# Keys of both attentions in parts of 72, 72 and 128, and the indexer's heads issued in pairs

## The chip, the cores and the metric

The kernel runs on one core of a Trainium2 chip. The metric is the device time of one execution in microseconds (us). TensorE (PE in the profile) multiplies; its weight loads have rows of their own (PEld). VectorE (DVE), ScalarE (ACT) and GpSimd (POOL) do the rest, and SyncE (SP) issues the weight transfers.

## The reference, cut to what matters

A decoder block works on 272 positions, 16 meta tokens and 256 real ones. A sparse attention and a forgetting attention, 8 heads of 128 each, run in parallel; a mixture of 16 experts follows. For the real positions it comes to:

```python
# sparse attention (A): the indexer scores the keys, the best 68 stay
dots  = einsum('bqhd,bsd->bqhs', qi, ki)              # 16 heads of 64
score = einsum('bqh,bqhs->bqs', wi, relu(dots)) * 64 ** -0.5
_, sel = lax.top_k(where(causal, score, NEG), 68)
ya = softmax(q @ k_sel.T * 128 ** -0.5) @ v_sel       # 8 heads
# forgetting attention (B): all earlier keys, with a decay
yb = softmax(where(causal, q @ k.T * 128 ** -0.5 + cq - c, NEG)) @ v
merged = sigmoid(ga) * (ya @ w_branch_a) + sigmoid(gb) * (yb @ w_branch_b)
h = h + merged @ w_out
h = h + hier_moe(h)                                   # 16 experts
```

## The kernel before

Weights come as pieces of 1 MB by SP's queue (`Stream.load`). In the projections each half of a piece is split by ACT (`whi`, line 132) and DVE (`wlo`, line 133), and `projT` (line 286) issues three products for each tile of 128 weight columns. Every `projT` step ends in `tick()`, and `later(d, f)` puts `f` into the tick `d` steps on. So indexer and attentions stand on TensorE's queue in small blocks between blocks of 24 projection products (48 between two ticks in which attention B has work). A scheduler behind the program orders each engine's instructions by what is ready. A float32 product counts as two passes in the profile, each with its weight load; a transpose and a product of a split operand count as one.

The **indexer** (`index_dots`, line 509): `qiT` holds the queries of two heads of 64 on the two partition halves, and `kiT` holds the keys twice. A dot product of query tile `t` (0 or 1) and head `h` contracts over 64 partitions, those of the half `h % 2`, and streams 144 keys (`t` = 0) or 272 (`t` = 1). ACT takes the relu, DVE adds it into `score[t]`. Tick `1 + i` issues head `i` for both query tiles, so both products of a tick use the same half. PSUM has two buffers (`psx`), which lie in different banks.

The **attentions** (`attention`, line 545) go through 16 steps (2 query tiles of 8 heads), each of three parts in following ticks (every second tick in B): `s1` makes logits (`pqk`) and the softmax on DVE and ACT (lines 557 to 562); `s2` transposes the probabilities into one PSUM tile (`ppt`) and ACT copies them to SBUF; `s3` multiplies by the values into `pav`. The 272 keys are cut into the 16 meta tokens and two blocks of 128; query tile 0 sees 16 + 128 keys, tile 1 all three parts. The first product of `s3` therefore contracts over 16 partitions (`vm`, `pTm`), the others over 128. The values are brought into that form by `v_out` (line 478), again with transposes of 128, 128 and 16 columns. The meta values of both attentions share the tile `vmeta`, on partitions 0 to 15 and 32 to 47.

After the attentions come the rest of the gated projections, the output projection (`wo`), the routing, and the experts (`up_unit`, `down_unit`), whose weights use 11 and later 12 more buffers.

Of the kernel before, what the change touches and what calls it, by code (L numbers as in the profile page):

```python
# [8 lines left out]
F32 = mybir.dt.float32  # L9
# [4 lines left out]
AF = mybir.ActivationFunctionType  # L14
# [7 lines left out]
TOPK = 68  # L22
EPS = 1e-6
NEG = -1e30
TAKEN = -3e38
CAP = 64
SPLITS, LOOK = 5, 3
# [122 lines left out]
def hybrid_block(ctx, tc, a):  # L150
    nc = tc.nc
    V, S, T = nc.vector, nc.scalar, nc.tensor
# [7 lines left out]
    U1 = ctx.enter_context(tc.tile_pool(name="units", bufs=4))  # L160
    ph1 = ExitStack()
    U2 = ph1.enter_context(tc.tile_pool(name="units2", bufs=9))
    tmp = ph1.enter_context(tc.tile_pool(name="tmp", bufs=1))

    def unit(shape, dt, name, pool=U1):
        return pool.tile(shape, dt, name=name, tag="u")

    def pj(shape, name="pj"):
        return ps.tile(shape, F32, name=name, tag="pj", bufs=4)

    def psx(shape, name="psx"):
        return ps.tile(shape, F32, name=name, tag="psx", bufs=2)

    def pt(shape, name="pt"):
        return ps.tile(shape, F32, name=name, tag="pt", bufs=1)

    def pv(shape, name="pv"):
        return ps.tile(shape, F32, name=name, tag="pv", bufs=1)

    def mm(out, lhsT, rhs, start, stop):  # L180
        T.matmul(out, lhsT, rhs, start=start, stop=stop, skip_group_check=True)  # L181
# [26 lines left out]
    ident = const.tile([128, 128], F32, name="ident")  # L208
# [20 lines left out]
    def row272(rows=128):  # L229
        return tmp.tile([128, L], F32, name="row", tag="row", bufs=5)[:rows]  # L230
# [37 lines left out]
    def later(d, f, *args):  # L268
        clock[1] += 1
        todo.append((clock[0] + d, clock[1], f, args))  # L270
# [36 lines left out]
    rrow = tmp.tile([128, L], F32, name="rrow")  # L307
# [109 lines left out]
    foxr = tmp.tile([104, L], F32R, name="foxr")  # L417
# [35 lines left out]
    causal = [tmp.tile([128, NK[t]], F32, name=f"causal{t}") for t in range(2)]  # L453
    for t in range(2):
        V.tensor_scalar(causal[t], jp[:, :NK[t]], 16 + 128 * t, NEG, op0=OP.is_gt, op1=OP.mult)

# [7 lines left out]
    for j in range(4):  # L464
        p = projT(16, xreal, 256)
# [2 lines left out]


    kaT = unit([128, 8, L], F32, "kaT", U2)  # L470
    va = unit([128, 2, 1024], F32, "va", U2)
    vmeta = tmp.tile([48, 1024], F32, name="vmeta")
    vam, vbm = vmeta[0:16], vmeta[32:48]

    def cks(k):
        return ckT[0][:, k, :], ckT[1][:, k, :]

    def v_out(c, p, v, vm, row):

        o = row272()  # L480
        if row is None:
            V.tensor_copy(o, p)
        else:
            V.tensor_tensor(o, p, row, op=OP.mult)
        hs = slice(c * 128, c * 128 + 128)

        def tr():
            q = (pv if c % 2 else pt)([128, 3, 128], "pvt")
            for t in range(2):
                T.transpose(q[:, t, :], o[:, 16 + t * 128:144 + t * 128], ident)  # L490
            T.transpose(q[:16, 2, :], o[:, 0:16], ident)
            S.activation(v[:, :, hs], q[:, 0:2, :], AF.Copy)
            S.activation(vm[:, hs], q[:16, 2, :], AF.Copy)
        later(1, tr)

    for j in range(4):
        p = projT(4, cks, L)
        for i in range(2):
            ropeT_to(kaT[:, 2 * j + i, :], p[i], ropeT[0], ropeT[1], 64)
    for j in range(4):  # L500
        p = projT(4, cks, L)
        for i in range(2):
            v_out(2 * j + i, p[i], va, vam, None)


    score = [tmp.tile([128, 4 + NK[t]], F32, name=f"score{t}") for t in range(2)]
    maskA = [tmp.tile([128, NK[t]], F32, name=f"maskA{t}") for t in range(2)]
# [11 lines left out]
    def topk_round(t):  # L519
        m = tmp.tile([128, 8], F32, name="max8", tag="max8", bufs=2)  # L520
        V.max(m, score[t])
        V.match_replace(score[t], m, score[t], TAKEN)

    def topk_mask(t):
        V.tensor_scalar(maskA[t], score[t][:, 4:], 0.5 * TAKEN, NEG, op0=OP.is_gt, op1=OP.mult)
        V.tensor_tensor(maskA[t], maskA[t], causal[t], op=OP.add)
# [1 line left out]
    for t in range(2):  # L528
        V.memset(score[t][:, 0:4], 3e38)
    for i in range(16):  # L530
        later(1 + i, index_dots, 0, i)
        later(1 + i, index_dots, 1, i)
    for t in range(2):
        for r in range(9):
            later(18 + r // 2 + 5 * t, topk_round, t)
# [2 lines left out]
    qaT = unit([128, 8, 256], F32, "qaT", U2)  # L538
    for j in range(4):
        p = projT(16, xreal, 256)  # L540
# [1 line left out]
            ropeT_to(qaT[:, 2 * j + i, :], p[i][:, :256], tabq[0], tabq[1], 64)  # L542


    def attention(qT, kT, v, vm, masks, yTh, yTl, extra, start, step, mb):
        n = 0
        accs = {}
        for t in (0, 1):
            for h in range(8):
                def s1(t=t, h=h):  # L550
                    nk = NK[t]
                    p = psx([128, L], "pqk")
                    mm(p[:, :nk], qT[:, h, t * 128:(t + 1) * 128], kT[:, h, :nk], True, extra is None)
                    if extra is not None:
                        mm(p[:, :nk], extra[0](t, h), extra[1][:, :nk], False, True)
                    lg = row272()
                    V.tensor_tensor(lg[:, :nk], p[:, :nk], masks[t], op=OP.add)
                    st4 = tmp.tile([128, 4], F32, name="st4", tag="st4", bufs=4)
                    V.tensor_reduce(st4[:, 0:1], lg[:, :nk], axis=AX.X, op=OP.max, negate=True)
                    S.activation(lg[:, :nk], lg[:, :nk], AF.Exp, bias=st4[:, 0:1], accum_out=st4[:, 1:2])  # L560
                    V.reciprocal(st4[:, 2:3], st4[:, 1:2])
                    V.tensor_scalar(lg[:, :nk], lg[:, :nk], st4[:, 2:3], None, op0=OP.mult)
                    later(step, s2, t, h, lg)

                def s2(t, h, lg):
                    q = pt([128, 3, 128], "ppt")
                    T.transpose(q[:16, 0, :], lg[:, 0:16], ident)
                    for b in range(t + 1):
                        T.transpose(q[:, 1 + b, :], lg[:, 16 + b * 128:144 + b * 128], ident)
                    pT = tmp.tile([128, 2, 128], F32, name="pT", tag="pT", bufs=2)  # L570
                    pTm = tmp.tile([48, 128], F32, name="pTm", tag="pTm", bufs=2)[mb:mb + 16]
                    S.activation(pTm, q[:16, 0, :], AF.Copy)
                    S.activation(pT[:, :t + 1, :], q[:, 1:2 + t, :], AF.Copy)
                    later(step, s3, t, h, pT, pTm)

                def s3(t, h, pT, pTm):
                    if h % 4 == 0:
                        accs[t] = pv([128, 4, 128], "pav")
                    o = accs[t][:, h % 4, :]
                    hs = slice(h * 128, h * 128 + 128)  # L580
                    mm(o, vm[:, hs], pTm, True, False)
                    for b in range(t + 1):
                        mm(o, v[:, b, hs], pT[:, b, :], False, b == t)
                    if h % 4 == 3:
                        g, c = slice(h - 3, h + 1), slice(t * 128, t * 128 + 128)
                        S.activation(yTh[:, g, c], accs[t], AF.Copy)
                        V.tensor_tensor(yTl[:, g, c], accs[t], yTh[:, g, c].bitcast(F32), op=OP.subtract)
                later(start + n * step, s1)
                n += 1

    def y_parts(n, pool):
        return unit([128, 8, 256], F32R, n + "h", pool), unit([128, 8, 256], F32R, n + "l", pool)


    vb = unit([128, 2, 1024], F32, "vb")
    for j in range(4):
        p = projT(16, xall, L)
        for i in range(2):
            v_out(2 * j + i, p[i], vb, vbm, rrow)
    yaTh, yaTl = y_parts("ya", U1)  # L600
    attention(qaT, kaT, va, vam, maskA, yaTh, yaTl, None, 1, 1, 0)

    kbT = unit([128, 8, L], F32, "kbT", U2)
    for j in range(4):
        p = projT(16, xall, L)
        for i in range(2):
            V.tensor_tensor(kbT[:, 2 * j + i, :], p[i], rrow, op=OP.mult)
    qbT = unit([128, 8, 256], F32, "qbT")
    for j in range(4):
        p = projT(16, xreal, 256)  # L610
# [8 lines left out]
        return o  # L619

    ybTh, ybTl = y_parts("yb", U2)
    attention(qbT, kbT, vb, vbm, causal, ybTh, ybTl, (fox_lhs, foxr), 1, 2, 32)
    merged = [unit([128, 8, 256], F32, f"merged{i}", U2) for i in range(2)]
    mTh, mTl = [], []

# [33 lines left out]
    tmp = ctx.enter_context(tc.tile_pool(name="tmp2", bufs=1))  # L659
# [50 lines left out]
    for j in range(4):  # L710
        cs = slice(j * 512, (j + 1) * 512)
        p = [pj([128, 512]) for _ in range(2)]
# [34 lines left out]
    lg = sm([2, 24], "lgr")  # L747
    V.memset(lg[:, :, 20:24], TAKEN)
    for t in range(2):
        V.scalar_tensor_tensor(lg[:, t, 0:20], pr[:, t, :], rh[:, t:t + 1], brb, op0=OP.mult, op1=OP.add)  # L750

    def best(src, name):
# [4 lines left out]
        for t in range(2):  # L757
# [8 lines left out]
    V.tensor_tensor(ng, i4, g4, op=OP.not_equal)  # L766
    V.scalar_tensor_tensor(lge.rearrange("p t (g e) -> p t g e", g=4), ng[:, :, :, None].to_broadcast([128, 2, 4, 4]), TAKEN,
                           lg[:, :, 0:16].rearrange("p t (g e) -> p t g e", g=4), op0=OP.mult, op1=OP.add)
# [69 lines left out]
    hs = {}  # L838
# [113 lines left out]
    for kind, n, i in UNITS:  # L952
        if kind == "u":
            g, j = n // 4, n % 4 * 4 + i
# [46 lines left out]
    with tc.If(more > 0):  # L1001
        with tc.tile_pool(name="fb", bufs=1) as fb:
# [3 lines left out]
            q = pt([128, 256], "pfr")  # L1006
# [12 lines left out]
            with tc.For_i(0, 16, 1) as e:  # L1019
# [4 lines left out]
                for s in range(2):  # L1024
                    p = [pj([128, 2, 256], "pfh") for _ in range(2)]
# [91 lines left out]
```

## Time and profile before

| | |
|---|---|
| median of 3 runs | 1250.81 us (1250.37 to 1253.12) |
| profiled execution | 1254.03 us, its span 1252.4 us |
| PE busy | 1198.1 us (96%) |
| PEld, DVE, ACT busy | 70%, 47%, 37% of the span |
| mean bandwidth | 265 GB/s |

The busy share of PE tells which engine to look at, not whether it works at full rate: a pass that waits for its weights counts as busy. What a block costs is read from the starts of the passes in the timeline.

### The profile page before, as it was taken

To read this page: it belongs to the slowest core of one execution; us is meant where nothing else is said; L and a number is where in the kernel's file an instruction comes from. 1 tells how busy PE (TensorE), PEld (TensorE's weight loads), DVE (VectorE), ACT (ScalarE), POOL (GpSimd) and SP (SyncE) were. 2 spreads that over 40 slices of the span, in tenths; PEclk is the share of its full clock that TensorE was granted. 3 is DMA by queue.
4 is the path that set the end of the run, shared out by engine and by line. 5 is a ranking of instruction groups with operands and counts; after the bars stand their busy time and mean duration, and the time that the engine had idled before them with its cause. 6 is when DMAs were issued, how large, how long until landed. Compare 5 with 4: busy or idle time off the path is not lost.

```text
span 1252.4 us, 18527 instructions
## 1 busy us (share of the span) xinstructions
PE 1198.1 (96%) x7602; PEld 878.7 (70%) x7602; DVE 593.5 (47%) x1075; ACT 461.4 (37%) x792; POOL 23.9 (2%) x31
## 2 busy tenths in 40 slices
PE   6999999999999999999999998999999999999994
PEld 6999889999999999999998875443433343333331
DVE  7768868555555655566564435232313131211212
ACT  6567644444355654444444324221211121000013
POOL 1000000000000000000000000000000000000002
PEclk9999999999999999999999998999999999999997
DMA  7554334433543444555559944999999999999992
GB/s 259 199 175 166 135 135 169 160 110 112 179 182 139 148 152 152 185 193 178 200 192 422 383 156 159 420 422 421 420 422 421 420 420 422 422 422 421 421 401 71
DMA packets 48456, 331.41 MB, mean 265 GB/s; under 512 B 5584, under 2 KB 6240, under 8 KB 9200
## 3 DMA queue, kind: packets, MB, share of 16 engines
q1 hardware_dynamic: 47088, 324.88, 66.2%
q0 software_dynamic: 1136, 5.29, 1.1%
q8 instruction: 62, 1.02, 0.3%
q14 instruction: 26, 0.21, 0.0%
q10 hardware_dynamic: 144, 0.01, 0.0%
HBM read 325.96 MB, written 4.19 MB: 264 GB/s over the span
## 4 chain that ended last, share of the span: by engine, by line
PE 92%; ACT 3%; DVE 3%; issue 1%; DMA 1%; SPq 0%; ACTq 0%
PE pj L181 50%; PE pgu L181 19%; PE py L181 10%; PE pxg L181 3%; PE pco L181 3%; PE pav L181 2%; PE pidx L181 1%; PE pqk L181 1%; ACT yh L916 1%; DVE yl L917 1%; PE prt L181 1%; DMA raw<-in_w 1%; ACT xTh L255 1%; PE psm L181 0%; DVE act L891 0%
## 5 line engine op out<-in xcount | busy, mean ns | idle before, releaser
L133 DVE TENSOR_TENSOR wlo<-raw,whi 128x1024 fp32r<-128x1024 f32 (+1 forms) x227 | 276.9, 1223 | 196.6 <-ACT whi L132 195.4
L181 PE MATMUL pj<-xTh,whi 128*128 128x256 f32 (+1 forms) x1216 | 348.0, 286 | 9.9 <-ACT xTh L255 9.9
L132 ACT ACTIVATE whi<-raw 128x1024 fp32r<-128x1024 f32 (+1 forms) x227 | 237.9, 1053 | 324.2 <-PE pj L181 297.1
L181 PE MATMUL pj<-xTl,whi 128*128 128x256 f32 (+1 forms) x1216 | 343.7, 283 | 0.0
L181 PE MATMUL pj<-xTh,wlo 128*128 128x256 f32 (+1 forms) x1216 | 342.6, 282 | 0.2 <-DVE wlo L133 0.2
L181 PE MATMUL pgu<-raw,xg 128*64 128x512 f32 x1024 | 263.2, 600 | 0.0
L181 PEld LDWEIGHTS pj<-xTh,whi 128*128 128x128 f32 x1216 | 229.5, 189 | 14.3 <-ACT xTh L255 9.9
L181 PEld LDWEIGHTS pj<-xTh,wlo 128*128 128x128 f32 x1216 | 229.1, 188 | 1.3 <-DVE wlo L133 0.5
L181 PEld LDWEIGHTS pj<-xTl,whi 128*128 128x128 f32 x1216 | 229.5, 189 | 0.7 <-issue 0.4
L181 PEld LDWEIGHTS pgu<-raw,xg 128*64 128x64 f32 x1024 | 77.8, 137 | 141.2 <-issue 137.7
L181 PE MATMUL py<-raw,aT 128*64 128x512 f32 x512 | 141.4, 603 | 0.5 <-ACT aT L903 0.5
L917 DVE TENSOR_TENSOR yl<-py,yh 128x512 fp32r<-128x512 f32 x32 | 22.1, 692 | 154.0 <-ACT yh L916 154.0
L181 PEld LDWEIGHTS py<-raw,aT 128*64 128x64 f32 x512 | 43.3, 138 | 71.1 <-issue 69.1
L916 ACT ACTIVATE yh<-py 128x512 fp32r<-128x512 f32 x32 | 19.1, 598 | 158.8 <-PE py L181 101.7
L891 DVE SCALAR_TENSOR_TENSOR act<-pgu,gsl,su 64x512 f32<-64x512 f32 x16 | 12.0, 750 | 98.7 <-ACT su L890 98.7
L890 ACT ACTIVATE su<-pgu 64x512 f32<-64x512 f32 x16 | 9.5, 592 | 131.5 <-PE pgu L181 131.5
L846 ACT ACTIVATE hsh<-hx,rh 128x256 fp32r<-128x256 f32 x64 | 30.4, 500 | 71.1 <-PE pxg L181 65.6
L847 DVE SCALAR_TENSOR_TENSOR hsl<-hx,rh,hsh 128x256 fp32r<-128x256 f32 x64 | 29.3, 479 | 49.0 <-ACT hsh L846 49.0
L181 PE MATMUL pj<-whi,mTh 128*128 128x512 f32 x128 | 51.0, 398 | 0.0
L181 PE MATMUL pj<-whi,mTl 128*128 128x512 f32 x128 | 50.5, 395 | 0.0
L181 PE MATMUL pj<-wlo,mTh 128*128 128x512 f32 x128 | 50.5, 394 | 0.0
L928 DVE TENSOR_TENSOR hx<-pco,hx 128x512 f32<-128x512 f32 x64 | 41.2, 686 | 18.5 <-PE pco L181 18.2
(293 smaller groups left out, 1389.4 us busy)
## 6 DMA issues: line engine op xcount, KB each, us to landing
raw<-in_w SPq DMA_DIRECT2D x303, 1024.0 KB, 15.7
hx<-in_x POOLq DMA_DIRECT2D x2, 1024.0 KB, 13.3
hTd<-y POOLq DMA_DIRECT2D x8, 256.0 KB, 5.5
out_dram<-hgf SPq DMA_DIRECT2D x8, 256.0 KB, 4.2
xr<-in_xT SPq DMA_DIRECT2D x3, 544.0 KB, 8.5
raw<-in_w SPq DMA_DIRECT2D x4, 256.0 KB, 7.0
raw<-in_w SPq DMA_DIRECT2D x2, 512.0 KB, 8.6
gfin<-in_g_final POOLq DMA_DIRECT2D x1, 1024.0 KB, 10.0
```

Of the source, the lines that this page charges most:

```text
L132: self.nc.scalar.activation(hi[:, c], src[:, c], AF.Copy)
L133: self.nc.vector.tensor_tensor(lo[:, c], src[:, c], hi[:, c].bitcast(F32), op=OP.subtract)
L181: T.matmul(out, lhsT, rhs, start=start, stop=stop, skip_group_check=True)
L255: S.activation(h, x, AF.Copy, scale=g)
L846: S.activation(h[:, t, :], x, AF.Copy, scale=rh[:, t:t + 1])
L847: V.scalar_tensor_tensor(l[:, t, :], x, rh[:, t:t + 1], h[:, t, :].bitcast(F32), op0=OP.mult, op1=OP.subtract)
L890: S.activation(su, p[half(e + 1)], AF.Silu)
L891: V.scalar_tensor_tensor(x, p[half(e)], gsl[e // 2][half(e)], su, op0=OP.mult, op1=OP.mult)
L916: S.activation(h, y, AF.Copy)
L917: V.tensor_tensor(l, y, h.bitcast(F32), op=OP.subtract)
L928: V.tensor_tensor(x, q, x, op=OP.add)
```

## The change

The keys are cut at 72 and 144 (`KEYS`): tile 0 has two parts of 72, tile 1 these and one of 128. The number of transposes, products and passes stays the same. The values of the third part get a tile of their own (`va2`, `vb2`, in place of `vmeta`), and the probabilities of a step go into one tile `pT` of three parts: ACT copies 72 x 256 at once, and for tile 1 another 128 x 128. In the indexer a tick issues two neighbouring heads of one query tile, tile 0 and tile 1 in turn.

```diff
+KEYS = ((0, 72), (72, 72), (144, 128))
@@ v_out
-            for t in range(2):
-                T.transpose(q[:, t, :], o[:, 16 + t * 128:144 + t * 128], ident)
-            T.transpose(q[:16, 2, :], o[:, 0:16], ident)
-            S.activation(v[:, :, hs], q[:, 0:2, :], AF.Copy)
-            S.activation(vm[:, hs], q[:16, 2, :], AF.Copy)
+            for i, (k, n) in enumerate(KEYS):
+                T.transpose(q[:n, i, :], o[:, k:k + n], ident)
+            S.activation(v[0][:72, :, hs], q[:72, 0:2, :], AF.Copy)
+            S.activation(v[1][:, hs], q[:, 2, :], AF.Copy)
@@ indexer
     for i in range(16):
-        later(1 + i, index_dots, 0, i)
-        later(1 + i, index_dots, 1, i)
+        for h in (i // 2 * 2, i // 2 * 2 + 1):
+            later(1 + i, index_dots, i % 2, h)
@@ attention, s2
-                    T.transpose(q[:16, 0, :], lg[:, 0:16], ident)
-                    for b in range(t + 1):
-                        T.transpose(q[:, 1 + b, :], lg[:, 16 + b * 128:144 + b * 128], ident)
...
-                    S.activation(pTm, q[:16, 0, :], AF.Copy)
-                    S.activation(pT[:, :t + 1, :], q[:, 1:2 + t, :], AF.Copy)
+                    for i, (k, m) in enumerate(KEYS[:t + 2]):
+                        T.transpose(q[:m, i, :], lg[:, k:k + m], ident)
+                    pT = tmp.tile([128, 3, 128], F32, name="pT", tag="pT", bufs=2)
+                    S.activation(pT[:72, :2, :], q[:72, :2, :], AF.Copy)
+                    if t:
+                        S.activation(pT[:, 2, :], q[:, 2, :], AF.Copy)
@@ attention, s3
-                    mm(o, vm[:, hs], pTm, True, False)
-                    for b in range(t + 1):
-                        mm(o, v[:, b, hs], pT[:, b, :], False, b == t)
+                    for i, (k, m) in enumerate(KEYS[:t + 2]):
+                        w = v[1][:, hs] if i == 2 else v[0][:m, i, hs]
+                        mm(o, w, pT[:m, i, :], i == 0, i == t + 1)
```

## Rows read from the trace of the kernel before

**Rows 1.** The page, part 4: shares of the chain that ended last, by engine.

```profile
PE 92%; ACT 3%; DVE 3%; issue 1%; DMA 1%; SPq 0%; ACTq 0%
```

**Rows 2.** Windows (indexer, attention A): us, busy PE, PEld, DVE, ACT, POOL, PEclk, DMA.

```profile
119.43:183.29 63.86, 63.57 (x458) 55.36 (x455) 45.60 (x88) 34.96 (x72) 0.00 (x0) 1.00 0.37 136
237.20:313.47 76.27, 75.72 (x562) 69.31 (x560) 43.77 (x92) 36.59 (x90) 0.00 (x0) 1.00 0.33 117
```

**Rows 3.** Waits (total us, times, longest): SP's queue; weight loads, 790 to 1230 us.

```profile
SPq L113 <- PE pgu L181: 195.3, 93, 21.6
...
PEld pgu L181 <- DMA raw<-in_w: 0.9, 3, 0.4
```

**Rows 4.** Timeline (start us, us), PE: a tick of attention A, query tile 0.

```profile
249.05 0.27 PE L567 MATMUL ppt<-ident,row 128*16 128x128 f32 x1
249.16 0.27 PE L569 MATMUL ppt<-ident,row 128*128 128x128 f32 x1
249.37 0.48 PE L181 MATMUL pav<-pTm,vmeta 16*128 16x128 f32 x2
249.78 0.49 PE L181 MATMUL pav<-pT,va 128*128 128x128 f32 x2
250.02 0.37 PE L181 MATMUL pj<-xTh,whi 128*128 128x272 f32 x1
```

**Rows 5.** Timeline, PE: attention A, query tile 1, the two blocks of 128 keys.

```profile
285.58 0.71 PE L181 MATMUL pav<-pT,va 128*128 128x128 f32 x4
286.05 0.37 PE L181 MATMUL pj<-xTh,whi 128*128 128x272 f32 x1
```

**Rows 6.** Timeline, PE: the logits of attention B, with a product of 104 rows.

```profile
355.70 0.41 PE L181 MATMUL pqk<-kbT,qbT 128*128 128x144 f32 x2
355.85 0.33 PE L181 MATMUL pqk<-foxr,lhf 104*128 104x144 f32 x1
356.01 0.32 PE L181 MATMUL pj<-xTh,whi 128*128 128x256 f32 x1
```

**Rows 7.** Timeline, PE: a regular tick of the indexer (144 twice, 272 twice; first form named).

```profile
162.85 0.97 PE L181 MATMUL pidx<-kiT,qiT 64*128 64x144 f32 x4
163.75 0.38 PE L181 MATMUL pj<-xTh,whi 128*128 128x256 f32 x1
```

**Rows 8.** Timeline, PE: the two places where one dot product stands alone.

```profile
137.80 0.51 PE L181 MATMUL pidx<-kiT,qiT 64*128 64x144 f32 x2
138.24 0.39 PE L181 MATMUL pj<-xTh,wlo 128*128 128x256 f32 x1
...
141.47 0.72 PE L181 MATMUL pidx<-kiT,qiT 64*128 64x272 f32 x2 [0.21 <-ACT row L515]
142.12 0.38 PE L181 MATMUL pj<-xTh,wlo 128*128 128x256 f32 x1
```

**Rows 9.** Tile pidx between 139.36 and 139.40 (ns, starts, forms); timeline of the place.

```profile
L181 PE MATMUL pidx<-kiT,qiT x2: 387/440/493, 139.1 to 139.4; 64*128 64x272 f32 x1, 64*128 64x144 f32 x1
...
139.12 0.75 PE L181 MATMUL pidx<-kiT,qiT 64*128 64x272 f32 x4
139.80 0.39 PE L181 MATMUL pj<-xTl,whi 128*128 128x256 f32 x1
```

**Rows 10.** Windows of tile pidx: us, busy PE, PEld, ACT, PEclk, DMA, in one stretch.

```profile
137.50:146.70 9.20, 3.96 (x16) 2.25 (x16) 2.97 (x10) 1.00 0.34 126
```

**Rows 11.** Timeline: the tightest softmax of A, the split after it, its transposes.

```profile
307.26 0.36 DVE L562 TENSOR_SCALAR row<-row,st 128x272 f32<-128x272 f32 x1
...
308.39 1.06 ACT L132 ACTIVATE whi<-raw 128x1024 fp32r<-128x1024 f32 x1 [1.36 <-PE pj L181]
...
308.30 0.27 PE L567 MATMUL ppt<-ident,row 128*16 128x128 f32 x1
```

**Rows 12.** The chain in order of time (start us, us): 46 passes of the experts, twice.

```profile
1027.06 10.46 PE pgu L181 x46
...
1089.45 12.06 PE pgu L181 x46
```

More of the change, by code (lines that the diff above doesn't have):

```diff
@@ L470, in hybrid_block, with values, v_out @@
     kaT = unit([128, 8, L], F32, "kaT", U2)
-    va = unit([128, 2, 1024], F32, "va", U2)
-    vmeta = tmp.tile([48, 1024], F32, name="vmeta")
-    vam, vbm = vmeta[0:16], vmeta[32:48]
+    def values(n, pool):
+        return unit([128, 2, 1024], F32, n, pool), tmp.tile([128, 1024], F32, name=n + "2")
+    va = values("va", U2)
     def cks(k):
         return ckT[0][:, k, :], ckT[1][:, k, :]
-    def v_out(c, p, v, vm, row):
+    def v_out(c, p, v, row):
         o = row272()
@@ L502, in hybrid_block @@
         for i in range(2):
-            v_out(2 * j + i, p[i], va, vam, None)
+            v_out(2 * j + i, p[i], va, None)
     score = [tmp.tile([128, 4 + NK[t]], F32, name=f"score{t}") for t in range(2)]
@@ L542, in hybrid_block, with attention @@
             ropeT_to(qaT[:, 2 * j + i, :], p[i][:, :256], tabq[0], tabq[1], 64)
-    def attention(qT, kT, v, vm, masks, yTh, yTl, extra, start, step, mb):
+    def attention(qT, kT, v, masks, yTh, yTl, extra, start, step):
         n = 0
@@ L566, in s2, with s3 @@
                     q = pt([128, 3, 128], "ppt")
-                    T.transpose(q[:16, 0, :], lg[:, 0:16], ident)
-                    for b in range(t + 1):
-                        T.transpose(q[:, 1 + b, :], lg[:, 16 + b * 128:144 + b * 128], ident)
-                    pT = tmp.tile([128, 2, 128], F32, name="pT", tag="pT", bufs=2)
-                    pTm = tmp.tile([48, 128], F32, name="pTm", tag="pTm", bufs=2)[mb:mb + 16]
-                    S.activation(pTm, q[:16, 0, :], AF.Copy)
-                    S.activation(pT[:, :t + 1, :], q[:, 1:2 + t, :], AF.Copy)
-                    later(step, s3, t, h, pT, pTm)
-                def s3(t, h, pT, pTm):
+                    for i, (k, m) in enumerate(KEYS[:t + 2]):
[4 more added lines that the diff above has]
+                        S.activation(pT[:, 2, :], q[:, 2, :], AF.Copy)
+                    later(step, s3, t, h, pT)
+                def s3(t, h, pT):
                     if h % 4 == 0:
@@ L592, in y_parts @@
         return unit([128, 8, 256], F32R, n + "h", pool), unit([128, 8, 256], F32R, n + "l", pool)
-    vb = unit([128, 2, 1024], F32, "vb")
+    vb = values("vb", U1)
     for j in range(4):
@@ L598, in hybrid_block @@
         for i in range(2):
-            v_out(2 * j + i, p[i], vb, vbm, rrow)
+            v_out(2 * j + i, p[i], vb, rrow)
     yaTh, yaTl = y_parts("ya", U1)
-    attention(qaT, kaT, va, vam, maskA, yaTh, yaTl, None, 1, 1, 0)
+    attention(qaT, kaT, va, maskA, yaTh, yaTl, None, 1, 1)
     kbT = unit([128, 8, L], F32, "kbT", U2)
@@ L621, in hybrid_block @@
     ybTh, ybTl = y_parts("yb", U2)
-    attention(qbT, kbT, vb, vbm, causal, ybTh, ybTl, (fox_lhs, foxr), 1, 2, 32)
+    attention(qbT, kbT, vb, causal, ybTh, ybTl, (fox_lhs, foxr), 1, 2)
     merged = [unit([128, 8, 256], F32, f"merged{i}", U2) for i in range(2)]
```

## The prediction

> **What bounds the kernel now.** First comes the chain that ended last: 92% of it is TensorE [rows 1], so a change pays where it shortens TensorE's own stream. Then the windows of the two stretches that the change touches: in the indexer's 63.86 us TensorE is busy 63.57 us, in attention A's 76.27 us 75.72 us, at a granted clock of 1.00 (2.4 GHz), with VectorE and ScalarE well below [rows 2]. Busy time can't tell whether those passes run at full rate, so the third view is the timeline of single ticks, where the distance between starts is what a pass costs [rows 4 to 9]. Last the waits, for whether time won early reaches the end: SP's longest wait for TensorE is 21.6 us, the load that stands until the first expert products free a buffer, and the experts' products wait 0.9 us in all for weights [rows 3]. So transfers start when TensorE lets them, and the experts keep their length. What is won before them arrives at the end.
>
> **Attentions: the product over 16 keys.** In the tick of query tile 0 [rows 4] the two transposes start 0.11 us apart, although one has 16 columns. Then the distances jump. The first 16-row pass starts 0.21 us after the last transpose. Its pair lasts 0.41 us (249.37 to 249.78), and the pair over 128 rows 0.24 us (249.78 to 250.02). Undisturbed distances: with tile 1 the four passes over 128 rows take 0.47 us [rows 5], where two take 0.24, so a further pass costs 0.115 us; and two full-array passes ahead of a pass of another kind take 0.15 us (355.70 to 355.85) [rows 6]. So going into 16 rows and back costs 0.21 - 0.11 = 0.10 at the entry, 0.41 - 2 x 0.115 = 0.18 inside, and 0.24 - 0.15 = 0.09 on the way out, together 0.37 to 0.38 us. In the row for 104 contracted rows nothing of this is seen: from the full pair into it and out again it is 0.15 and 0.16 us [rows 6]. 72 rows are not in the trace. They lie between 64, which does pay (below), and 104, which doesn't; also above half the array, and so I put them with 104. Both ends stay: nothing saved, or 0.38 us for each of 2 x 16 steps. I take 32 x 0.38 = **12.2 us**; rounding of the starts leaves 11.5 to 12.8.
>
> The rest of this part I cost at nothing on TensorE: passes and transposes keep their number, and 16 columns or 128 in a transpose made no difference [rows 4]. ScalarE does one copy less in a step of tile 0 and as many in tile 1, and its queue has room [rows 2]. No transfer is added and SP's order stays. What could come late is the softmax, as each tick gets 0.38 us shorter. In the tightest place DVE ends at 307.62 and the transposes start at 308.30 [rows 11]: 0.68 us in hand, 0.30 afterwards. No new wait.
>
> **Indexer: which half.** A regular tick runs four passes over 64 rows, 0.90 us up to the next projection product [rows 7]. A dot product alone takes 0.44 us over 144 keys and 0.65 over 272 [rows 8]. In both kernels a tick goes into 64 rows once and comes back once; the new question is whether two heads on the two halves run side by side. The trace holds one such place. From 139.12 on, a 272 pair and a 144 pair of neighbouring heads met, and all four passes were through in 0.68 us (139.80), hardly more than the 272 pair alone. At 139.40 one pass of each had started, so the second head didn't wait for the second pass of the first [rows 9]. Hence a tick of two heads costs what one head costs alone: two ticks (one per query tile) take 0.44 + 0.65 = 1.09 us where they took 2 x 0.90 = 1.80, which saves 0.71 us, eight times: **5.7 us**. Four of the sixteen ticks are not regular: their 16 passes are squeezed into 137.5 to 146.7 us [rows 10], as the dot products met late buffers. 1.4 us of the 5.7 hang on them. If all eight came one at a time, three runs more than now at 1.09 - 0.90 = 0.19 us, it would be -0.6; in four clean pairs, with one run less than now, about 2.1. So 3.7 to 6.4, and I take the middle of the regular price.
>
> TensorE dispatching passes strictly in order would give less. The Trainium skill, TensorE: Matmul & The Clock Gate, Part 3, "What overlaps and what doesn't", says that products start and end in program order and only weight loads overtake, and then only on other rows. The row at 139.40 speaks against the first half here: a later head's pass had started ahead of the earlier head's second. By the skill's rule the sum would be the first rival's.
>
> VectorE and ScalarE have the same work in the stretch: 45.60 us of 63.86 for VectorE [rows 2], 78% of 58.2, so TensorE stays the bound. Buffers of a tick are as many as before.
>
> **Sum.** 12.2 + 5.7 = 17.9 us. The profiled run, 1254.03 us with a span of 1252.4, would go to 1236.1. It stands 3.2 us above the median of the runs; the same cut from the median 1250.81 gives **1232.9 us**.
>
> **Rivals.** (1) Passes in order: the second head's first pass only goes beside the first head's second. A pass over 144 keys is (0.65 - 0.44) / 256 x 144 = 0.12 us, over 272 it is 0.22. The two ticks take 1.09 + 0.12 + 0.22 = 1.43 us and save 0.37, 3.0 us in all. If the second head's weights also load in the open (0.44 - 2 x 0.12 = 0.20 us for load and exit, about half each), it is 0.17 a pair, 1.4 us. So 2.2 in the middle: 1250.8 - 12.2 - 2.2 = 1236.4 us, or 1238.6 with no overlap at all. For it: rows 9 are one place. Against it: they contradict it.
> (2) 72 rows count as a part of the array like 16 and 64, and the steps keep their jumps. Only the indexer gains: 1245.1 us. Against it: the 104 rows [rows 6].
> (3) Neither part does what it says: 72 rows pay and the halves don't overlap, 1250.8 us.
> (4) Slower: the softmax of attention A falls behind the split. The scheduler orders ScalarE's queue, and with changed copies the exponential may be put behind `whi`, which waits for TensorE itself (308.39 in rows 11). It ends at 309.45; with the scaling alone (0.36) the transposes would start at 309.81 instead of 307.92, 1.9 us later. Sixteen heads lose 30 us: 1263 us. It decides once ten heads are hit (17.9 / 1.9 = 9.4). Against it: the steps keep their ticks, and the split's place in a tick is unchanged.
>
> Beyond these, the same 46 expert passes took 10.46 us in one place and 12.06 in another [rows 12]. One such place more or less is 1.6 us, and where they fall may shift when all else comes earlier.
>
> **How the numbers follow.** My forecast 0.68, rival 1 0.20, rival 2 0.05, rival 3 0.03, rival 4 0.04. The forecast's own bounds are 11.5 + 3.7 = 15.2 and 12.8 + 6.4 = 19.2, that is 1231.6 to 1235.6; with 1.6 on the lower side 1230.0. The upper end takes in rival 1 with its bounds and stops at 1239.0: 1230.0 to 1239.0. About 0.2% or 2.5 us is what a measurement here can tell from no change. Faster: forecast and rivals 1 and 2, 0.93. Same: rival 3, 0.03. Slower: rival 4, 0.04.
>
> **What would show it.** Right: in the timeline the `pav` passes follow the transposes at 0.11 us each, and A's stretch of 76.27 us shrinks by 16 x 0.38 = 6.1 us. An indexer tick lasts 0.44 and 0.65 us in turn, and its stretch shrinks by 5.7 us. Expert ticks are as long as before. Wrong: distances of 0.2 us around the 72-row passes (rival 2); index ticks near 0.56 to 0.67 and 0.87 to 0.98 us (rival 1); waits of `ppt` for DVE in every tick (rival 4); an experts' stage that lengthens by what was won.

## The result, and the profile after

The changed kernel takes 1238.02 us (median of 4 runs, 1234.9 to 1238.53), the kernel before in the same comparison 1251.96 us. The ratio is 0.9879 with a 95% interval of 0.9863 to 0.9895: 13 to 17 us less. The prediction was 1232.9 us in a range of 1230.0 to 1239.0, so the time lies near the upper end. The profiled executions, whose traces are compared below, go from 1254.03 to 1237.73 us, and their spans from 1252.4 to 1236.1: 16.3 us. In the experiments below one run of `same_half` took 1348.56 us at a mean granted clock of 0.845, against 0.989 to 0.991 in its other five, and is left out of that kernel's time.

TensorE still sets the end. The same line of the page that [rows 1] shows is now:

```profile
PE 90%; ACT 4%; DVE 4%; issue 1%; DMA 0%; SPq 0%; ACTq 0%
```

The windows of the three stretches that the change touches show where the time went. Columns: stretch, its length, busy time of PE, PEld, DVE, ACT, POOL, clock, DMA share, GB/s. The indexer is taken here from its first pass to the projection pass after its last, attention A from the projection pass behind the first logits, attention B from its first logits; both attentions end at the projection pass after the last product. (The expectations below measure the indexer from its first pass to its last: 59.9 us before, 56.5 after.) First the kernel before:

```profile
123.10:183.28 60.18, 59.89 (x425) 51.92 (x424) 44.30 (x86) 32.84 (x67) 0.00 (x0) 1.00 0.36 129
...
237.22:313.47 76.25, 75.70 (x562) 69.29 (x560) 43.77 (x92) 36.57 (x90) 0.00 (x0) 1.00 0.33 117
355.70:478.55 122.85, 122.85 (x987) 117.34 (x985) 72.16 (x137) 74.26 (x125) 0.00 (x0) 1.00 0.42 149
```

And the changed kernel:

```profile
122.44:179.23 56.79, 55.89 (x426) 48.77 (x425) 45.70 (x90) 32.57 (x67) 0.00 (x0) 1.00 0.38 132
...
233.14:303.02 69.88, 69.72 (x561) 68.25 (x560) 43.92 (x92) 35.45 (x82) 0.00 (x0) 1.00 0.35 124
345.24:462.08 116.84, 116.84 (x986) 116.12 (x985) 72.06 (x137) 70.14 (x117) 0.00 (x0) 1.00 0.44 157
```

The indexer lost 3.4 us, attention A 6.4 and attention B 6.0, 15.8 us together. Another 0.7 us lies before the indexer, which starts at 122.44 instead of 123.10; that is scatter and not the change, since the start lies between 122.44 and 123.78 in the profiles of this study, at 123.10 before, at 123.17 with the attentions' part alone and at 122.96 when the changed kernel was profiled again. TensorE finished attention B 16.5 us earlier, and the span is 16.3 us shorter. From the first pass of the experts to the end it is 490.2 us before and 490.7 after: what was won went through to the end.

In the timeline of attention A (start us, length us) the jumps of [rows 4] are gone, for query tile 0 and, lower, for tile 1:

```profile
244.22 0.38 PE L569 MATMUL ppt<-ident,row 128*72 128x128 f32 x2
244.44 0.61 PE L182 MATMUL pav<-pT,va 72*128 72x128 f32 x4
244.81 0.38 PE L182 MATMUL pj<-xTh,whi 128*128 128x272 f32 x1
...
272.46 0.49 PE L569 MATMUL ppt<-ident,row 128*72 128x128 f32 x3
272.79 0.83 PE L182 MATMUL pav<-pT,va 72*128 72x128 f32 x6
273.38 0.37 PE L182 MATMUL pj<-xTh,whi 128*128 128x272 f32 x1
```

Transposes and products now stand 0.11 us apart throughout: two transposes and four passes take 0.59 us (244.22 to 244.81), where the same six took 0.97 (249.05 to 250.02 in [rows 4]). That is 0.38 us a step, as worked out. It holds in every step: all 32 pairs over 16 rows have their passes 0.21 us apart in the trace of before, and after the change all distances between passes over 72 rows are 0.11 us.

An indexer tick with two heads on the two halves, over 272 and over 144 keys:

```profile
150.17 0.73 PE L182 MATMUL pidx<-kiT,qiT 64*128 64x272 f32 x4
150.83 0.39 PE L182 MATMUL pj<-xTh,whi 128*128 128x256 f32 x1
...
153.85 0.52 PE L182 MATMUL pidx<-kiT,qiT 64*128 64x144 f32 x4
154.29 0.38 PE L182 MATMUL pj<-xTh,whi 128*128 128x256 f32 x1
```

They last 0.66 and 0.44 us, as one dot product alone did in [rows 8]. The tile view of the first of them, between 150.165 and 150.20 us (durations in ns, then first and last start), shows two passes begun by then, one of each head; of two heads on one half only one has (`same_half`, below):

```profile
L182 PE MATMUL pidx<-kiT,qiT x2: 493/493/493, 150.2 to 150.2; 64*128 64x272 f32 x2
```

### The profile page after: what moved, and what is told of

It reads as the page before. It is cut to its first block, busy times and chain, and to the rows that moved or that the text cites. A ratio compares the mean times of both kernels' runs of the same rounds, so it can differ in the third digit from the quotient of the medians.

```text
span 1236.1 us, 18505 instructions
## 1 busy us (share of the span) xinstructions
PE 1182.1 (96%) x7602; PEld 873.1 (71%) x7602; DVE 594.3 (48%) x1075; ACT 455.7 (37%) x776; POOL 23.9 (2%) x31
## 4 chain that ended last, share of the span: by engine, by line
PE 90%; ACT 4%; DVE 4%; issue 1%; DMA 0%; SPq 0%; ACTq 0%
PE pj L182 49%; PE pgu L182 19%; PE py L182 10%; PE pxg L182 3%; PE pco L182 3%; PE pav L182 1%; PE pqk L182 1%; ACT yh L916 1%; PE ppt L569 1%; DVE wlo L134 1%; DVE yl L917 1%; PE pidx L182 1%; PE prt L182 1%; ACT xTh L256 1%; PE psm L182 0%
## 5 line engine op out<-in xcount | busy, mean ns | idle before, releaser
L182 PEld LDWEIGHTS py<-raw,aT 128*64 128x64 f32 x512 | 42.9, 136 | 69.9 <-issue 67.0
```

## Experiments

Each time stands beside that of the kernel before on the same chip. There were three groups of runs, in which its medians were 1253.35, 1252.96 and 1251.17 us; across groups the ratios are to be compared.

### Each half of the change alone

The attentions alone: the changed kernel with the old loop of the indexer.

```diff
-        for h in (i // 2 * 2, i // 2 * 2 + 1):
-            later(1 + i, index_dots, i % 2, h)
+        later(1 + i, index_dots, 0, i)
+        later(1 + i, index_dots, 1, i)
```

> The attention half of the change alone; the indexer issues its heads as before. Theory: the whole gain of the attentions is the removed jumps around the 16-row products, 0.38 us in each of 32 steps, and it passes to the end: 12.2 us faster than before, near 1239.5 us, attention A's stretch 6.1 us shorter. Rival: part of it is given back in the experts' stage, then the time is above 1242 although A and B shrink.

Measured: 1241.95 us against 1253.35, ratio 0.9916 (0.9902 to 0.9930). Windows of the indexer and of attention A:

```profile
123.17:183.36 60.19, 59.92 (x426) 51.92 (x425) 44.31 (x86) 32.89 (x67) 0.00 (x0) 1.00 0.36 129
237.29:307.15 69.86, 69.69 (x561) 68.22 (x560) 43.94 (x92) 35.48 (x82) 0.00 (x0) 1.00 0.35 125
```

The indexer is as long as before the change, attention A as short as after it, and the span falls from 1252.4 to 1240.3 us: 12.1 us. The medians give 11.4 and the ratio 10.5; against the two runs of the kernel before at 0.988, the mean granted clock of all five runs of `att_only`, it is 12.1 again. The time stands close to the rival's 1242, but the experts take 490.7 us, as after the full change: nothing is given back.

The indexer alone: the kernel before with the new loop.

```diff
-        later(1 + i, index_dots, 0, i)
-        later(1 + i, index_dots, 1, i)
+        for h in (i // 2 * 2, i // 2 * 2 + 1):
+            later(1 + i, index_dots, i % 2, h)
```

> The indexer half alone; keys stay at 16, 128 and 128. In the changed kernel the indexer's stretch shrank by 3.4 us, not 5.7. Theory: the regular ticks give 0.71 us a pair, and the irregular stretch near 126 to 146 us, where buffers are late, takes 2.3 us back; that has nothing to do with the attentions, so 3.4 us here too, near 1248.5 us. Rival: the attentions' part made the irregular stretch worse, then 5 to 6 us here.

Measured: 1247.89 us against 1253.35, ratio 0.9963 (0.9950 to 0.9977). Its indexer stretch:

```profile
123.78:180.55 56.77, 55.86 (x425) 48.74 (x424) 45.70 (x90) 32.55 (x67) 0.00 (x0) 1.00 0.38 133
```

It is 3.4 us shorter than before, the same as in the full change, and attention A stays at 76.25 us. So the missing 2.3 us have nothing to do with the attentions. The time itself fell by 5.5 us in the medians and 4.6 in the ratio, more than 3.4; all its five runs had a mean clock of 0.991, and against the eight runs of the kernel before at that clock (median 1250.76) it is 2.9. What these clocks are is told under what was not expected.

### What makes a product expensive: the rows it contracts over

`keys64` keeps everything but the cut: 64, 80 and 128.

```diff
-KEYS = ((0, 72), (72, 72), (144, 128))
+KEYS = ((0, 64), (64, 80), (144, 128))
@@ v_out and s2: 80 columns and rows for both small parts, so that copies keep their number
-                T.transpose(q[:n, i, :], o[:, k:k + n], ident)
+                n = max(n, 80)
+                T.transpose(q[:n, i, :], o[:, k:k + n], ident)
```

> The changed kernel with keys in parts of 64, 80 and 128: the same numbers of transposes, passes and copies (the transposes of the first part bring 80 columns, of which 64 are used). Theory: a product over 64 rows or fewer puts the array into another division, and going there and back costs 0.38 us, whether it is 16 rows or 64; over 72 or 80 rows it stays whole. The jumps of 0.2 us are back in all 32 steps, 12 us lost, near 1248 to 1250 us. Rival: the cost came from the smallness of 16 rows, or from mixed sizes as such; then 64 rows cost little and it stays near 1238.

Measured: 1250.51 us against 1253.35, ratio 0.9987 (0.9976 to 0.9997), and 12.5 us above the changed kernel's 1238.02 of another group (by the ratios 13.5). Timeline of a step of query tile 0:

```profile
245.11 0.38 PE L571 MATMUL ppt<-ident,row 128*80 128x128 f32 x2
245.43 0.90 PE L182 MATMUL pav<-pT,va 64*128 64x128 f32 x4
246.09 0.37 PE L182 MATMUL pj<-xTh,whi 128*128 128x272 f32 x1
```

From the first transpose to the projection pass it is 0.98 us again, with 64 rows as with 16, and attention A takes 76.08 us. So it is not the smallness of 16 that costs: 16 and 64 rows pay the same, 72, 80 and 104 pay nothing of their own (where 80 rows pay here, it is for coming back from 64; with tile 1 the first 128-row pass starts 0.11 us after the last one over 80). What lies between 65 and 71 was not tried.

### What makes the indexer faster: the two halves

`same_half` issues two heads of one query tile in a tick, as the changed kernel does, but two that lie on the same half.

```diff
-        for h in (i // 2 * 2, i // 2 * 2 + 1):
+        for h in (i // 4 * 4 + i // 2 % 2, i // 4 * 4 + i // 2 % 2 + 2):
```

> The changed kernel, but the two heads of an indexer tick lie on the same half of the array (heads 0 and 2, 1 and 3, ...), still of one query tile. Theory: the gain of the indexer is that the two halves run side by side; on one half a tick costs 0.68 us (144 keys) and 1.12 us (272), 1.80 a pair as before the change, so a regular pair loses the 0.71 us: 4 to 5 us slower than the changed kernel, near 1241 to 1242. Rival: the gain came from issuing two products of one query tile, then it stays near 1238.

Measured: 1241.39 us, ratio 0.9906 (0.9891 to 0.9921). Two ticks, and the tile view of the first between 151.71 and 151.76 us:

```profile
151.72 1.18 PE L182 MATMUL pidx<-kiT,qiT 64*128 64x272 f32 x4
152.83 0.38 PE L182 MATMUL pj<-xTh,whi 128*128 128x256 f32 x1
...
155.84 0.75 PE L182 MATMUL pidx<-kiT,qiT 64*128 64x144 f32 x4
156.52 0.38 PE L182 MATMUL pj<-xTh,whi 128*128 128x256 f32 x1
...
L182 PE MATMUL pidx<-kiT,qiT x1: 493/493/493, 151.7 to 151.7; 64*128 64x272 f32 x1
```

The ticks last 1.11 and 0.68 us, 1.79 a pair as before the change (1.80), and the indexer's stretch is 60.66 us, 3.9 more than with the changed kernel and 0.5 more than before the change. Two products of one query tile bring nothing by themselves; the gain is the two halves.

### Where 2.3 us of the indexer went

The stretch shrank by 3.4 us instead of 5.7, while its regular ticks are as short as forecast. The loss is in the first 25 us. ScalarE's relus in the trace of the changed kernel, from 126 us on:

```profile
136.37 0.40 ACT L516 ACTIVATE row<-pidx 128x272 f32<-128x272 f32 x1
137.78 0.37 ACT L516 ACTIVATE row<-pidx 128x272 f32<-128x272 f32 x1
139.82 0.29 ACT L516 ACTIVATE row<-pidx 128x144 f32<-128x144 f32 x1 [1.67 <-DVE score L518]
```

The two dot products of the second tick, multiplied from 125.90 us on, get their relus at 136.37 and 137.78. In between `fox_logs`, which makes the decay for attention B, takes all five buffers of the tile `row` for a long chain on VectorE and ScalarE. The first relu starts as line 440 ends, the last reader of one of these five buffers:

```profile
135.96 0.37 DVE L440 TENSOR_TENSOR row<-row 8x272 f32<-8x272 f32 x1
```

The two PSUM buffers stay full, the scheduler puts 83 projection passes in a row, and the eight dots that piled up come afterwards in six runs, four of them single. The kernel before has the same 83 passes in a row, and then five runs. Two edits take this apart: more buffers at the same place, or the function at another time.

```diff
@@ rows8
-        return tmp.tile([128, L], F32, name="row", tag="row", bufs=5)[:rows]
+        return tmp.tile([128, L], F32, name="row", tag="row", bufs=8)[:rows]
@@ fox_late
-    later(26, fox_logs)
+    later(76, fox_logs)
```

The changed kernel itself ran again beside them.

> The changed kernel once more, beside the next three on one chip. The stretches should stand as in its first profile: indexer 56.5 us from its first pass to its last, attention A 70.0, B 116.8. What differs from run to run should lie in the experts' stage alone, where stretches at half clock fall or don't: 490.7 us from the first expert pass to the end with 6.8 us of half clock, about 487 without.

Measured: 1238.51 us (1235.05 to 1238.75) against 1252.96, ratio 0.9882 (0.9862 to 0.9903). The stretches stand as expected: 56.4 us from the indexer's first pass to its last, attention A 69.9, B 116.8, and 490.7 us from the first expert pass to the end with 6.8 us of half clock, though at other places than in the first profile.

> The changed kernel with eight buffers of the tile row instead of five. In the irregular stretch the first 272-key pair of the indexer waits about 10 us for its relu: line 424's function for the decay holds all five buffers of row from 125 to 138 us. Theory: the missing buffers are the cause, with three more the relus go on and the indexer's stretch falls from 56.5 to 53.5 us, the length of fifteen regular ticks. Rival: VectorE's queue is the cause, with the decay's long operations ahead of the sums; then the stretch stays above 55.5 us.

Measured: 1235.31 us, ratio 0.9866 (0.9842 to 0.9889), and the indexer's stretch:

```profile
123.35:177.80 54.45, 54.45 (x425) 48.22 (x424) 45.24 (x89) 32.23 (x67) 0.00 (x0) 1.00 0.40 138
```

> The changed kernel with the function for the decay of attention B put 50 ticks later, into the projections of attention B's queries, where no tile row is in use. Buffers and VectorE's queue are then both free during the indexer. Theory (either cause): the indexer's stretch falls to 53.5 us, nothing else grows, 3.0 us faster than the changed kernel. Rival: the indexer's first ticks are late for another reason (the first sums wait for the keys); then the stretch stays at 56.5.

Measured: 1233.81 us (1232.1 to 1235.45), ratio 0.9858 (0.9839 to 0.9876). The indexer and attention A, and below the relus at the old place:

```profile
123.26:177.04 53.78, 53.78 (x426) 47.82 (x425) 36.46 (x67) 28.16 (x62) 0.00 (x0) 1.00 0.39 140
230.95:300.66 69.71, 69.71 (x561) 68.27 (x560) 46.44 (x99) 37.78 (x85) 0.00 (x0) 1.00 0.35 122
...
127.73 0.67 ACT L516 ACTIVATE row<-pidx 128x272 f32<-128x272 f32 x2
131.39 0.45 ACT L516 ACTIVATE row<-pidx 128x144 f32<-128x144 f32 x2
```

Of the stretch's 56.79 us, three more buffers take off 2.3 and the later function 3.0, and TensorE has no idle time left in either (53.78 of 53.78). So buffers were most of it; the last 0.7 us is the function's own work on VectorE or what three buffers still don't hold, which the two runs don't part. The relus follow in their ticks, and attention A is no longer. (The medians lie 4.7 us apart, but two of the four runs of `fox_late` had the mean clock of 0.991 and one of the changed kernel's; compared at like clocks it is 2.7 and 3.3.)

Did the decay cost the kernel before as much?

```diff
@@ the kernel before
-    later(26, fox_logs)
+    later(76, fox_logs)
```

> The kernel before, with the function for the decay 50 ticks later. In the kernel before the indexer's stretch is 59.9 us where fifteen regular ticks of 3.91 us and one block take 59.2, so the decay there costs only about 0.7 us; in the changed kernel it cost 3.0. Theory: the decay holds the buffers for the same time in both, but the old ticks left it room. The stretch falls by 0.7 us to 59.2. Rival: the decay costs the old kernel as much as the new one, and old regular ticks elsewhere are misjudged; then it falls by 2 us or more.

Measured: 1252.78 us against 1251.17, ratio 1.0004 (0.9991 to 1.0016): no difference to be told in the time. Its indexer:

```profile
123.44:182.92 59.48, 59.48 (x425) 51.80 (x425) 34.78 (x63) 28.45 (x62) 0.00 (x0) 1.00 0.37 131
```

60.18 to 59.48 is 0.7 us, as expected. Without the decay in the way, the new order of heads saves 59.48 - 53.78 = 5.70 us, the forecast figure; with it, 3.4, because the same obstacle costs 3.0 instead of 0.7.

### Not dividing the array at all

"Dividing" is the name used here for what the traces show around products over 16 or 64 rows, the jumps between starts; how the array is arranged then no profile shows. `idx_pad` takes the indexer's products over all 128 rows. The keys stand in two tiles, each with zeros on one half.

```diff
-        b = (h % 2) * 64
-        mm(p[:, :n], qiT[b:b + 64, h // 2, t * 128:(t + 1) * 128], kiT[b:b + 64, :n], True, True)
+        mm(p[:, :n], qiT[:, h // 2, t * 128:(t + 1) * 128], kiT[h % 2][:, :n], True, True)
```

> The changed kernel, with the indexer's products taken over all 128 rows: two tiles of keys, each with zeros on one half, so the queries of the other head are multiplied by zero. Twice the useful rows, but the array is never divided. Theory: a pass costs 0.12 or 0.23 us like any other, a pair of ticks 1.40 us of passes against 1.48 with the divided array, entry and exit counted; in the irregular stretch, where dots come alone, each run saves 0.38 us more. Together 0.6 to 2.5 us off the indexer's stretch of 56.5. Rival: going into 64 rows costs nothing to speak of when both halves run, then the padded passes cost 0.35 us a tick more and the stretch is 5 us longer.

Measured: 1236.29 us, ratio 0.9869 (0.9849 to 0.9889). The two regular ticks:

```profile
150.41 1.08 PE L182 MATMUL pidx<-kiT,qiT 128*128 128x272 f32 x4
151.13 0.48 PE L182 MATMUL pj<-xTh,whi 128*128 128x256 f32 x1
...
154.14 0.65 PE L182 MATMUL pidx<-kiT,qiT 128*128 128x144 f32 x4
154.53 0.38 PE L182 MATMUL pj<-xTh,whi 128*128 128x256 f32 x1
```

0.72 and 0.39 us up to the next projection pass, against 0.66 and 0.44 on the halves, and the way in is shorter (0.11 us from the pass before, 150.30 to 150.41, where the halves take 0.20). The stretch is 56.06 us, 0.7 less. That is the lower end of what was expected. The likely reason, argued and not shown, is that in the irregular part the dots wait for buffers, so that a run without an entry gains little there. The medians lie 2.2 us apart, at like clocks 0.4 to 0.8.

> The changed kernel with the later decay and the indexer over 128 rows with zeros, the two edits that shortened the stretch, together. With nothing late a regular pair of ticks is 7.03 us padded and 7.09 with the divided array, so the stretch should be 53.0 us, 0.4 under the later decay alone; in time that is within what runs differ. Rival: the padded form hides something that the irregular stretch hid too, and more than 1 us comes off.

Measured: 1233.99 us (1233.52 to 1234.91), ratio 0.9859 (0.9841 to 0.9877); the indexer's stretch is 53.23 us, 0.55 below `fox_late`. In time the two can't be told apart.

The fastest kernels of the study are the change with the later decay and its padded form. The former takes 1233.81 us beside 1238.51 for the change and 1252.96 for the kernel before.

## Why the prediction was right, point by point

**The bound, and the way to the end.** Right: TensorE's stream was shortened by 16.5 us up to the end of attention B, and the span by 16.3; the experts kept their length (490.2 and 490.7 us).

**Attentions, 12.2 us.** Right, in size and cause: 6.4 us in A (0.4 of it idle time that went) and 6.0 in B, 12.1 us of span in `att_only`. That 72 rows go with 104 and not with 16 was a guess between two rows of the trace; `keys64` shows that the line runs between 64 and 72, and that the jumps had nothing to do with small parts as such. The softmax kept its ticks, as argued.

**Indexer, 5.7 us.** The price of a pair of ticks was right: 0.66 + 0.44 = 1.10 us for the forecast 1.09. The step that failed is the one on the four irregular ticks, "I take the middle of the regular price": they were to bring 1.4 us and cost 0.9 (3.4 less the 4.3 of the twelve regular ones). The lower bound of -0.6 counted three more runs, but no waits for buffers: there was one run more, and TensorE's idle time in the stretch rose from 0.29 us (60.18 - 59.89) to 0.90 (56.79 - 55.89). The bound was also too narrow by its own terms: 0.19 us for a further run leaves out its way in (0.20 us behind the pass before instead of 0.11) and the slow start of what follows (0.22 us to the second projection pass, 142.12 to 142.34, instead of 0.11). The rows that I had showed the squeeze [rows 10] and even its releaser, a wait for a relu [rows 8]; I did not follow that relu to what it waited for. `rows8`, `fox_late` and `before_late` did, and 5.70 us is what the order of heads gives where nothing is in its way.

**Rival 1, passes in order.** Fell. Its tick over 272 keys would last 0.87 to 0.98 us and takes 0.66. It followed the rule of the Trainium skill, TensorE: Matmul & The Clock Gate, Part 3, "What overlaps and what doesn't", that products start in program order. The trace doesn't agree for float32 products on the two row halves: by 150.20 us, 0.03 after the first pass of one head, one pass of each of two heads had begun, while the first head's second pass was still to come. The profile shows starts and not the order on the queue; but one order for all places doesn't fit either. Here both first passes come before both second ones, and from 141.83 us on, where a 272-key product and a later 144-key one met, both passes of the later had started by 142.10 us and only one of the earlier.

**Rivals 2 to 4.** Rival 2 (72 rows pay) and rival 3 fell with the timeline of attention A. Rival 4 (the exponential behind the split) doesn't show: attention B has no idle time of TensorE, and attention A 0.16 us.

**From 17.9 to what was measured.** 17.9 less the 2.3 of the indexer is 15.6, and 15.1 is what the ratio says (1251.96 x 0.0121). The rest of the distance to 1238.0 lies in which runs were drawn: I subtracted from a median of three runs, 1250.81, two of which were as short as runs at a mean clock of 0.991, while three of the changed kernel's four runs had 0.988. The next section shows what that is worth.

**The range.** The time fell into it partly by luck. 1238.0 lies above the forecast's own bounds, 1231.6 to 1235.6, and 17.9 us is more than the measured 13 to 17. It is in the range because the upper end was set to take in rival 1, which fell. By the time alone rival 1 (1236.4 to 1238.6) would have done better than the forecast; only the timelines tell them apart.

## What to carry to other kernels

In this kernel a product over 16 or 64 rows among products over the whole array cost 0.38 us in getting there and back, more than its two passes of 128 columns (0.23): cut keys (or any contraction) so that no part falls to 64 rows, or fill the rows with zeros, which cost no more in the indexer. If small products must stay, issue two on different halves next to each other; here they ran side by side. And when a change packs work more tightly into a stretch, follow each irregular place in the old trace to the buffer that it waited for, since that obstacle may cost more afterwards than before.

## What the runs showed of the hardware that was not expected

**Half-filled and full cost the same.** Two heads on the two halves of the array are no faster than the same two over all 128 rows with zeros for the other head (1.10 and 1.11 us a pair of ticks up to the next pass).

**Stretches at half clock among the experts.** Runs of one kernel differ by 3 us or so in two groups. Beside `after_again` the kernel before took 1250.7 to 1251.3 us in runs whose mean granted clock was 0.991, and 1253.0 to 1253.8 where it was 0.989. The changed kernel took 1235.05 us at 0.991 and 1238.4 to 1238.8 at 0.988, so it is 16.0 us faster at 0.991 and 14.8 in the lower group (medians 1251.05, and 1253.41 against 1238.58). The traces show the place: the clock is 0.50 (1.2 GHz) for a few us after a pause in the experts' products. Windows of the changed kernel, the pause, the stretch behind it, and what follows:

```profile
945.00:951.70 6.70, 5.34 (x22) 1.74 (x18) 2.49 (x5) 0.97 (x2) 0.00 (x0) 0.99 1.01 421
951.70:958.30 6.60, 6.57 (x18) 2.62 (x20) 0.65 (x3) 0.00 (x0) 0.00 (x0) 0.50 1.02 421
958.30:966.00 7.70, 7.70 (x35) 2.51 (x32) 0.00 (x0) 0.00 (x0) 0.00 (x0) 0.99 1.01 421
```

The kernel before has the same kind of pause with a shorter drop behind it, at the second place of [rows 12], and, in the lower two lines, without a drop:

```profile
1082.60:1089.30 6.70, 5.32 (x24) 2.09 (x20) 2.70 (x5) 0.60 (x1) 0.00 (x0) 0.99 1.02 424
1089.30:1092.50 3.20, 3.20 (x9) 1.07 (x11) 0.31 (x2) 0.00 (x0) 0.00 (x0) 0.50 1.01 422
...
962.00:968.40 6.40, 5.02 (x23) 1.98 (x20) 2.35 (x5) 0.60 (x1) 0.00 (x0) 1.00 1.02 425
968.40:979.00 10.60, 10.60 (x48) 3.59 (x48) 0.31 (x2) 0.06 (x1) 0.00 (x0) 1.00 1.01 419
```

TensorE is busy for some 80% of each pause, and what follows runs at full or at half clock. A second such drop of 3.4 us comes at 1212.1 us in the kernel before, so that both kernels have 6.8 us of half clock in their experts and their profiles are compared alike. Ten of the twelve profiles of this study have these 6.8 us, in one piece or two; `idx_only` and `fox_late` have none. Where it falls is not set by the kernel alone: the changed kernel has it 206 us after its first expert pass in one profile, and 327 and 450 us after it in the other. From the first expert pass to the end it is 490.7 us in the profiled run of the changed kernel, and 487.0 in that of `idx_only`, which has no such stretch; that also is why `idx_only` looked better than its 3.4 us, all its runs having a mean clock of 0.991. Why all five were so, and all five of `att_only` at 0.988, is open, and so is whether a shorter pause would rid every run of the drop; neither was tried.
